# The first gate/up pair in seven products, and the last pair's forms beside the down units: a streaming encoder layer on one core

## The chip, the core and the metric

The kernel runs on one core of a Trainium2 chip. Its time is the device time of one execution in microseconds (us); of several runs the median is taken. A profile is one execution taken by the hardware profiler. The engines are TensorE (PE, with its weight loads as PEld), VectorE (DVE), ScalarE (ACT), GpSimd (POOL) and SyncE (SP), which here only issues DMAs. Every engine works through its own queue in order.

## The reference

One layer of an encoder trunk for 512 new prompt frames and 64 sample frames (576 columns in all), in fp32: a norm, an input projection, stick-breaking attention for eight heads beside a gated convolution, two output norms, an output projection with the residual, and then the part that the change touches:

```
h2 = rmsnorm(x, g_norm2)
x  = x + (silu(h2 @ w_gate) * (h2 @ w_up)) @ w_down      # D_MODEL 2048, D_FF 5632
```

The matrix products are held to fp32 accuracy. The kernel splits each operand into a high part (`float32r`) and a low part and takes three matmuls for each product of blocks: high x high, low x high, high x low.

## The kernel before

**Products.** Activations lie transposed: channels on the 128 partitions, the 576 frames in two halves of 288 (`HALVES`). A product of a weight block of 256 columns with all frames has two column tiles and two frame halves, and its rows come in pairs of tiles: a 2 x 2 by 2 x 2 block product. `run` computes it by seven products instead of eight (Winograd's form of Strassen's method). The products are numbered 1 to 7; products 1, 6, 5 and 3 accumulate in one bank (`psy`), 7 and 4 in another (`psw`), 2 in a third (`psx`). Between them ACT copies the bank (`kept`, line 428), so that a later addition can use the state at that point. One product over 2048 rows is 24 matmuls (8 row pairs x 3), so one unit is 168.

**Weights.** Raw columns come by DMA into two tiles of two halves each, `raw_a` and `raw_b` (`load_columns`, line 330), 1 MB a time. `weight_sums` (lines 347 to 353) forms the four sums of weight blocks on VectorE, and `prepare` splits one product's weights: a copy on ACT (line 231) and a subtraction on VectorE (line 232) into `whl`. It runs four products ahead.

**Frames.** The other operand of products 1, 2 and 3 are parts of the activations themselves (`h2a`, `b22s`); products 5 and 6 use the frame sums `t12`, products 7 and 4 the frame sums `t34`.

**Stages around the change.** `out_proj` runs twice: first over the convolution part, while the heads' attention runs between its steps, then over the attention part (799 to 901 us in the profile). In the second run each eviction multiplies by the row scale `Ra` and adds to the residual (lines 1005 and 1006), and `after_b2` makes the normed operand of the gate/up stage in high and low parts (lines 1248 and 1249) and sums squares (ACT line 1255, POOL line 1256). Then `wide` computes gate and up of the first column pair in eight products of 2 x 192 matmuls, with its own weight tiles, while `frame_sums` fills `t12` and `t34`. The row scale `R2` is formed in the middle of it (`row_scale2`). Then come 42 gate/up units (21 pairs) of seven products, then 37 down units. An activation `finish`es a gate or up quadrant: it is scaled by `R2`, the gate goes through Silu, and up is multiplied by gate.

**Forms.** The down units use seven products too, with the hidden activations as frames. So for each pair `put_forms` makes the seven frame forms (lines 1339, 231, 232) and stores each by DMA to `hid_dram` (line 1331, 288 KB), from SP, or from POOL for the last pair. `load_pair` brings a pair's forms back into one of seven slots (lines 1482 and 1490, 2 MB). The table `DOWN` says which row pairs a down unit covers: the first ones cover 3, 4, 5, 6 pairs, so a product of the first down unit is only 9 matmuls. The last pair's forms are first wanted by a unit near the end of the table.

**Order.** TensorE's order is written out by hand (`order`). Generators in a `Pipeline` advance at every step of three matmuls ("a tick"; `yield 9` waits nine). A planner sets the order on the other engines up to the last gate/up unit; from there on they follow the order of the text (`manual_schedule`).

Of the kernel before, what the change touches and what calls it, by code (L numbers as in the profile page):

```python
# [101 lines left out]
def tile_hybrid_stream_step(  # L102
# [47 lines left out]
    for w in (w_gate, w_up):  # L150
        for kk in range(2):
            specs.append((w[kk * 1024 : (kk + 1) * 1024, 0:256].rearrange("(k p) c -> p k c", p=P), 8, 256))
# [269 lines left out]
    def run(n, p_, early=False):  # L422
# [38 lines left out]
        elif p_ == 2:  # L461
            x = ps_z.tile([P, 512], F32, tag="z0", name="psx2")[:, :HALF]
            multiply(x, n, 2, True)
            add(0, 0, x, st["p1"])
# [531 lines left out]
    def out_proj(frame, R, after=None):  # L996
        for c in range(D // 256):
            whi, wlo = next_weight()
            load_x2()
            for j in range(2):  # L1000
                kt = 2 * c + j
                for a, b in HALVES:
                    ps = ps_pj.tile([P, HALF], F32, tag="pj", name="pjo")
                    product(ps, whi, wlo, slice(j * P, (j + 1) * P), frame, 8, a, b)
                    nc.vector.tensor_tensor(out=ps, in0=ps, in1=R[:, a:b], op=ALU.mult)
                    nc.vector.tensor_tensor(out=x2(kt)[:, a:b], in0=ps, in1=x2(kt)[:, a:b], op=ALU.add)
                if after:
                    after(kt)
# [225 lines left out]
    b12pool = tc.alloc_tile_pool(name="b12pool", bufs=1, reuse_waits="tile", side="left")  # L1234
    b12h = b12pool.tile([P, NP, HALF], F32R, name="b12h")
    b12l = b12pool.tile([P, NP, HALF], F32R, name="b12l")
    acc2 = [b12pool.tile([P, HALF], F32, name=f"acc2_{i}") for i in range(2)]

    def h2(kt, i):
        if i == 0:  # L1240
            return h2a[kt]
        return b22s[kt // 2] if kt % 2 else (b12h[:, kt // 2, :], b12l[:, kt // 2, :])

    def after_b2(kt):
        for i, (a, b) in enumerate(HALVES):
            hi, lo = h2(kt, i)
            src = x2(kt)[:, a:b]
            nc.scalar.activation(out=hi, in_=src, func=AF.Copy, scale=col("g2", kt))
            nc.vector.scalar_tensor_tensor(out=lo, in0=src, scalar=col("g2", kt), in1=hi.bitcast(F32),
                                           op0=ALU.mult, op1=ALU.subtract)  # L1250
# [6 lines left out]
        if kt % 4 == 3:  # L1257
            m = kt // 4
            for k in (4 * m, 4 * m + 2):
                nc.sync.dma_start(out=x2_dram[k : k + 2].rearrange("k p t -> p k t"), in_=x2t[k // 2])  # L1260

    out_proj(lambda k: mixa[k], Ra, after_b2)
    R2 = rpool.tile([P, T], F32, tag="R", name="R2", bufs=2)
    parts2 = []
    for i in range(2):
        sh, sl = parts("sq2")
        split(sh, sl, acc2[i])
        parts2.append((sh, sl))
# [13 lines left out]
    t34 = []  # L1282
# [5 lines left out]
    turn = [0]  # L1288

    def ps_tile(name):  # L1290
        turn[0] += 1
        if turn[0] % 2:
            return ps_pj.tile([P, HALF], F32, tag="pj", name=name)
        return ps_z.tile([P, 512], F32, tag=f"z{turn[0] // 2 % 3}", name=name)[:, :HALF]

    def frame_sums():

        for j in range(NP):
            ev, od = x2(2 * j), x2(2 * j + 1)
            ge, go = col("g2", 2 * j), col("g2", 2 * j + 1)  # L1300
            b11 = tmp.tile([P, HALF], F32, tag="ms", name="b11", bufs=1)
            b22 = tmp.tile([P, HALF], F32, tag="t", name="b22", bufs=1)
            nc.scalar.activation(out=b11, in_=ev[:, :HALF], func=AF.Copy, scale=ge)
            nc.scalar.activation(out=b22, in_=od[:, HALF:], func=AF.Copy, scale=go)
            ta = b12pool.tile([P, 2, HALF], F32, tag="ta", name="ta")
            tb = b12pool.tile([P, 2, HALF], F32, tag="tb", name="tb")
            t1, t2, t3, t4 = ta[:, 0], ta[:, 1], tb[:, 0], tb[:, 1]
            nc.vector.scalar_tensor_tensor(out=t1, in0=ev[:, HALF:], scalar=ge, in1=b11, op0=ALU.mult, op1=ALU.subtract)
            nc.gpsimd.tensor_tensor(out=t2, in0=b22, in1=t1, op=ALU.subtract)
            nc.vector.scalar_tensor_tensor(out=t3, in0=ev[:, HALF:], scalar=ge, in1=b22, op0=ALU.mult, op1=ALU.subtract)  # L1310
            nc.vector.scalar_tensor_tensor(out=t4, in0=od[:, :HALF], scalar=go, in1=t2, op0=ALU.mult, op1=ALU.subtract)
            two = t12[:, :, j] if j < NP - 1 else t12z
            split(two[:, :, 0, :], two[:, :, 1, :], ta)
            t34.append(ypool.tile([P, 2, 2, HALF], F32R, tag=f"y{j}", name=f"t34_{j}"))
            split(t34[j][:, :, 0, :], t34[j][:, :, 1, :], tb)
            yield 9

# [3 lines left out]
    spare = []  # L1321

    def put_form(fp, n, src):

        if fp == NFP - 1 and n > 3:
            t = spare.pop(0)()
        else:
            t = tmp.tile([P, 2, HALF], F32R, tag="hl", name="form")
# [28 lines left out]

    def finish(kind, fp, c, i, ps, part=None):
# [8 lines left out]
        else:  # L1367
            nc.vector.tensor_tensor(out=s, in0=ps, in1=part, op=ALU.add)  # L1368
            nc.vector.tensor_tensor(out=s, in0=s, in1=R2[:, a:b], op=ALU.mult)
        if kind == "gate":  # L1370
# [6 lines left out]
    def wide(kind, hold=None):  # L1377

        pss = {}
        for kk in range(2):  # L1380
            whi, wlo = next_weight()
            for i, j in ((1, 0), (1, 1), (0, 0), (0, 1)):
                if kk == 0:
                    pss[j, i] = ps_tile("pw")
                for k in range(8):
                    xh, xl = h2(8 * kk + k, i)
                    for n, (w_, x_) in enumerate(((whi, xh), (wlo, xh), (whi, xl))):
                        mm(pss[j, i], w_[:, k, j * P : (j + 1) * P], x_,  # L1388
                           start=(kk == 0 and k == 0 and n == 0), stop=(kk == 1 and k == 7 and n == 2))
                    pipe.tick()  # L1390
                if kk == 1:
                    finish(kind, 0, j, i, pss[j, i])
            if hold and kk == 0:
                hold()


    pipe.spawn(frame_sums(), 20)
    wanted += [(0, 0), (1, 0), (0, 1), (1, 1)] + [(n, c) for n in range(2, NGU) for c in range(2)]
    wanted += [(n, None) for n in range(NGU, NU)]
    wide("gate", row_scale2)  # L1400
    load_columns([("A", 0)])
    wide("up", lambda: load_columns([("A", 1)]))
    pipe.flush()
    b12pool.release()
# [3 lines left out]
    load_columns([("B", 0), ("B", 1)])  # L1408

# [191 lines left out]
```

## Time and profile before

| | |
|---|---|
| median of 3 runs | 2406.14 us (2406.02 to 2406.74) |
| profiled execution | 2408.49 us, span 2406.8 us |
| granted TensorE clock, mean | 0.994 |
| TensorE busy | 98% of the span, 17609 matmuls |
| VectorE, ScalarE, GpSimd busy | 81%, 51%, 12% |

A row of a group or of a timeline names line, engine, operation and tiles (written tile before the arrow, read tiles behind it) and the number of instructions. In a timeline the first number is the start and the second the time up to the end of the last instruction; matmuls follow each other more closely than they last, since they are pipelined. Square brackets give the idle time before and what ended it. In the table of stretches each engine has its busy time and number of instructions; the last columns are the granted clock, the DMA share and GB/s.

### The profile page before, as it was taken

The page shows a single profiled execution, that of the slowest core. Times are in us where ns is not written, and L with a number is a line of the kernel's source. Part 1 is how long each engine was busy: PE and PEld are TensorE (multiplying, and loading weights), DVE is VectorE, ACT ScalarE, POOL GpSimd, SP SyncE. Part 2 cuts the span into 40 slices and gives each one's busy share as a digit, 9 for nine tenths or more (in the row PEclk, how much of TensorE's full clock was granted, in tenths as well). Part 3 has the DMA queues.
Part 4 walks back from the last instruction along what each step waited for, and adds up shares of the span by engine and source line. Part 5 has one row for each costly group of instructions (what it writes and reads, how often), then busy time and mean ns, then how long its engine had stood idle before and what let it go on. Part 6 is the DMA issues. An engine that isn't in the chain of part 4 may idle for free.

```text
span 2406.8 us, 43812 instructions
## 1 busy us (share of the span) xinstructions
PE 2355.5 (98%) x17609; PEld 2339.5 (97%) x17609; DVE 1939.7 (81%) x2840; ACT 1235.0 (51%) x2207; POOL 298.9 (12%) x377
## 2 busy tenths in 40 slices
PE   8899999999999999999999999999999899999998
PEld 8899999998889999999999999999999899999998
DVE  7888898797677768888888888888888778887875
ACT  7456656455677545444444444444444444444454
POOL 0111121120233222000000000000000002431211
PEclk9999999999999999999999999999999999999999
DMA  7433342535632233535444444444444936885642
GB/s 253 140 113 108 108 140 86 161 99 184 224 107 89 100 127 118 155 112 158 150 128 145 146 143 132 144 150 141 129 152 141 339 112 205 221 226 195 205 128 79
DMA packets 474900, 360.60 MB, mean 150 GB/s; under 512 B 11278, under 2 KB 460680, under 8 KB 474696
## 3 DMA queue, kind: packets, MB, share of 16 engines
q1 hardware_dynamic: 469528, 351.02, 45.7%
q0 software_dynamic: 5168, 6.79, 1.6%
q8 instruction: 138, 2.26, 0.4%
q14 instruction: 66, 0.54, 0.1%
HBM read 281.39 MB, written 76.37 MB: 149 GB/s over the span
## 4 chain that ended last, share of the span: by engine, by line
PE 82%; DVE 6%; ACT 4%; issue 2%; POOL 2%; DMA 1%; SPq 0%; ACTq 0%; DVEq 0%; POOLq 0%
PE psy L405 43%; PE psw L405 21%; PE psx L405 10%; PE pjo L227 5%; DVE whl L232 1%; ACT whl L231 1%; PE pw L1388 1%; ACT ph L231 0%; PE psv L405 0%; PE pot L1511 0%; DVE c L866 0%; DVE raw_b L349 0%; POOL hbl L1117 0%; DMA raw_a<-in_w_down_dram 0%; DVE wlo L180 0%
## 5 line engine op out<-in xcount | busy, mean ns | idle before, releaser
L232 DVE TENSOR_TENSOR whl<-raw_a,whl 128x1024 fp32r<-128x1024 f32 (+4 forms) x376 | 426.4, 1135 | 69.4 <-ACT whl L231 67.8
L405 PE MATMUL psy<-t,whl 128*128 128x288 f32 x2916 | 438.4, 295 | 0.5 <-ACT part L428 0.5
L231 ACT CAST whl<-raw_a 128x1024 fp32r<-128x1024 f32 (+4 forms) x376 | 352.6, 938 | 137.9 <-PE psx L405 47.8
L405 PE MATMUL psy<-h_s,whl 128*128 128x288 f32 x2724 | 411.7, 295 | 6.8 <-ACT part L428 6.8
L405 PEld LDWEIGHTS psy<-t,whl 128*128 128x128 f32 x2916 | 403.7, 189 | 0.9 <-ACT part L428 0.7
L405 PEld LDWEIGHTS psy<-h_s,whl 128*128 128x128 f32 x2724 | 378.5, 189 | 7.3 <-ACT part L428 7.3
L405 PE MATMUL psw<-t,whl 128*128 128x288 f32 x2592 | 377.1, 295 | 0.0
L405 PEld LDWEIGHTS psw<-t,whl 128*128 128x128 f32 x2592 | 354.4, 189 | 0.2
L232 DVE TENSOR_TENSOR whl<-raw_b,whl 128x1024 fp32r<-128x1024 f32 (+5 forms) x230 | 248.7, 1081 | 86.4 <-ACT whl L231 85.1
L231 ACT CAST whl<-raw_b 128x1024 fp32r<-128x1024 f32 (+5 forms) x230 | 207.6, 904 | 206.9 <-PE psw L405 70.8
L428 ACT COPY part<-psy 128x288 f32<-128x288 f32 x303 | 121.2, 400 | 348.5 <-PE psy L405 346.4
L405 PE MATMUL psx<-h_s,whl 128*128 128x288 f32 x1122 | 165.1, 295 | 2.7 <-DVE gs L1368 2.7
L405 PEld LDWEIGHTS psx<-h_s,whl 128*128 128x128 f32 x1122 | 154.1, 188 | 2.9 <-issue 2.9
L231 ACT CAST whl<-s 128x1024 fp32r<-128x1024 f32 (+5 forms) x101 | 93.4, 924 | 119.9 <-PE psw L405 112.3
L405 PE MATMUL psy<-t12a,whl 128*128 128x288 f32 x1056 | 150.5, 295 | 3.1 <-ACT part L428 3.1
L405 PE MATMUL psw<-t34a,whl 128*128 128x288 f32 x1056 | 150.4, 295 | 2.1 <-DVE ghs L854 0.9
L405 PEld LDWEIGHTS psy<-t12a,whl 128*128 128x128 f32 x1056 | 143.5, 188 | 4.0 <-ACT part L428 4.0
L405 PEld LDWEIGHTS psw<-t34a,whl 128*128 128x128 f32 x1056 | 143.2, 188 | 2.7 <-DVE ghs L854 1.1
L227 PE MATMUL pjo<-mixc,whi 128*128 128x288 f32 x512 | 123.0, 307 | 1.2 <-ACT kcT L1063 1.2
L232 DVE TENSOR_TENSOR whl<-s,whl 128x1024 fp32r<-128x1024 f32 (+5 forms) x101 | 107.5, 1064 | 19.6 <-ACT whl L231 18.0
L1331 POOL DMA_DIRECT2D hid_dram<-form x3 | 2.4, 809 | 921.1 <-DVE form L232 921.1
L227 PE MATMUL pjo<-mixa,whi 128*128 128x288 f32 x512 | 102.1, 295 | 0.0
(599 smaller groups left out, 4146.8 us busy)
## 6 DMA issues: line engine op xcount, KB each, us to landing
hid_dram<-form SPq DMA_DIRECT2D x147, 288.0 KB, 2.3
raw_a<-in_w_gate_dram SPq DMA_DIRECT2D x23, 1024.0 KB, 6.2
raw_a<-in_w_up_dram SPq DMA_DIRECT2D x23, 1024.0 KB, 5.5
raw_a<-in_w_in_dram SPq DMA_DIRECT2D x22, 1024.0 KB, 5.5
raw_b<-in_w_in_dram SPq DMA_DIRECT2D x22, 1024.0 KB, 7.9
raw_b<-in_w_gate_dram SPq DMA_DIRECT2D x21, 1024.0 KB, 6.6
raw_b<-in_w_up_dram SPq DMA_DIRECT2D x21, 1024.0 KB, 7.7
h_s<-hid_dram SPq DMA_DIRECT2D x10, 2016.0 KB, 9.2
```

The lines of the kernel that those rows point to most:

```text
L227: mm(ps, w_[:, k, csl], x_[:, a:b], start=(k == 0 and n == 0), stop=(k == nk - 1 and n == 2))
L231: nc.scalar.copy(out=hi, in_=src)
L232: (lo_eng or nc.vector).tensor_tensor(out=lo, in0=src, in1=hi.bitcast(F32), op=ALU.subtract)
L405: mm(ps, whl[:, w_, j, :], x_, start=(start and j == 0 and q == 0), stop=(j == len(xs_) - 1 and q == 2), skip_group_check=True)
L428: nc.scalar.copy(out=t, in_=st["y"])
L1331: q.dma_start(out=hid_dram[fp][2 * n - 2 : 2 * n].rearrange("f p t -> p f t"), in_=t.bitcast(F32))
L1388: mm(pss[j, i], w_[:, k, j * P : (j + 1) * P], x_, start=(kk == 0 and k == 0 and n == 0), stop=(kk == 1 and k == 7 and n == 2))
```

## The change

The eight-product pair `wide`, its operand tiles and its weight loads go. All 22 pairs are units now, so there are 44 gate/up units. What they need at their start moves under the second `out_proj`:

- `frame_sums` is spawned for each pair of row tiles as soon as `out_proj` has finished it. `t34` goes where it went; `t12` cannot be written yet, as its memory still holds the attention operand, so each half goes to DRAM (`t12_dram`, 16 stores of 288 KB) and comes back in four loads when the projection has ended (`load_t12`).
- The columns of units 0 and 1 are loaded within the projection (`before_b2`), and the first two products of unit 0 are prepared there, with two of its weight sums.
- The start of `order` interleaves units 0 and 1, as the input projection's units do.
- `row_scale2` multiplies the sums of squares by ones in fp32 without splitting them, starts 19 ticks after the projection and takes the mean and the root in PSUM and on ACT. The first quadrant of unit 0 is finished six ticks late for it.
- For the last pair, `finish` leaves the quadrants that come last as they are, and `last_forms` does the rest: it starts 34 ticks later, beside the down units, and puts one form each ten ticks. The forms use the `hl` tiles instead of the down units' accumulators.

```diff
-    gu = [(kind, fp, 0, NP) for fp in range(1, NFP) for kind in ("gate", "up")]
+    gu = [(kind, fp, 0, NP) for fp in range(NFP) for kind in ("gate", "up")]
...
+    def frame_sums(j):
+        ev, od = x2(2 * j), x2(2 * j + 1)
...
+        nc.vector.scalar_tensor_tensor(out=t1, in0=ev[:, HALF:], scalar=ge, in1=b11, op0=ALU.mult, op1=ALU.subtract)
+        nc.gpsimd.tensor_tensor(out=t2, in0=b22, in1=t1, op=ALU.subtract)
+        nc.vector.scalar_tensor_tensor(out=t3, in0=ev[:, HALF:], scalar=ge, in1=b22, op0=ALU.mult, op1=ALU.subtract)
+        yield 4
+        nc.vector.scalar_tensor_tensor(out=t4, in0=od[:, :HALF], scalar=go, in1=t2, op0=ALU.mult, op1=ALU.subtract)
+        for q, t in enumerate((t1, t2)):
+            form = tmp.tile([P, 2, HALF], F32R, tag="hl", name="t12f")
+            split(form[:, 0], form[:, 1], t)
+            nc.sync.dma_start(out=t12_dram[q, j], in_=form.bitcast(F32))
+        yield 4
+        t34.append(ypool.tile([P, 2, 2, HALF], F32R, tag=f"y{j}", name=f"t34_{j}"))
+        for q, t in enumerate((t3, t4)):
+            split(t34[j][:, q, 0], t34[j][:, q, 1], t)
...
+        if kt % 2:
+            nc.sync.dma_start(out=x2_dram[kt - 1 : kt + 1].rearrange("k p t -> p k t"), in_=x2t[kt // 2])
+            pipe.spawn(frame_sums(kt // 2), 5)
+        if kt == KD - 2:
+            prepare(0, 1)
+            prepare(0, 2)
+            for _ in range(2):
+                one_sum(0)
+    def before_b2(c):
+        if c == 3:
+            load_columns([("B", 0), ("B", 1)])
+        elif c == D // 256 - 2:
+            load_columns([("A", 0)])
+        elif c == D // 256 - 1:
+            load_columns([("A", 1)])
...
     def row_scale2():
+        yield 19
         for i, (a, b) in enumerate(HALVES):
-            ss = channel_sums(*parts2[i], a, b, "ss2")
-            rsqrt_mean(R2[:, a:b], ss, D, HALF)
+            ss = misc("ss2")[:, :HALF]
+            mm(ss, oner.bitcast(F32), acc2[i], start=True, stop=True)
+            y, t = (tmp.tile([P, HALF], F32, tag=tag, name="y2") for tag in ("y", "r"))
+            nc.scalar.activation(out=ss, in_=ss, func=AF.Identity, scale=1.0 / D, bias=epsc)
+            nc.scalar.activation(out=y, in_=ss, func=AF.Ln)
+            nc.scalar.activation(out=y, in_=y, func=AF.Exp, scale=-0.5)
+            nc.scalar.activation(out=t, in_=y, func=AF.Square)
...
+    def load_t12():
+        yield 3
+        for q in (1, 0):
+            nc.sync.dma_start(out=t12[:, q].bitcast(F32), in_=t12_dram[q, : NP - 1].rearrange("j p f t -> p j f t"))
+            yield 6
+        for q in (1, 0):
+            nc.sync.dma_start(out=t12z[:, q].bitcast(F32), in_=t12_dram[q, NP - 1])
...
+    def last_forms(s10):
+        fp, h, tt = NFP - 1, hid.pop(NFP - 1), nc.vector.tensor_tensor
+        s00, s01, s11 = h[0, 0], h[0, 1], h[1, 1]
+        yield 34
+        tt(out=s01, in0=s01, in1=gates.pop((0, 1)), op=ALU.mult)
+        yield 5
+        tt(out=s10, in0=s10, in1=R2[:, :HALF], op=ALU.mult)
+        tt(out=s10, in0=s10, in1=gates.pop((1, 0)), op=ALU.mult)
+        for n, out, a, b in ((2, s10, None, None), (5, s00, s01, s00), (7, s01, s01, s11), (6, s11, s11, s00),
+                             (4, s10, s10, s11)):
+            yield 10
+            if a is not None:
+                tt(out=out, in0=a, in1=b, op=ALU.subtract)
+            put_form(fp, n, out)
...
-    wide("gate", row_scale2)
-    load_columns([("A", 0)])
-    wide("up", lambda: load_columns([("A", 1)]))
...
-    order = [(0, 1), (0, 2), (1, 1), (1, 2), (0, 6), (0, 7), (0, 5), (0, 3), (0, 4), (1, 6), (1, 7), (1, 5)]
-    for n in range(1, NU):
+    order = [(0, 1), (0, 2), (1, 1), (1, 2), (0, 3), (0, 6), (0, 5), (1, 3), (0, 7), (0, 4),
+             (1, 6), (1, 5), (1, 7), (2, 1), (1, 4), (2, 2), (2, 6), (2, 7), (2, 5)]
+    early = {0, 1}
+    for n in range(2, NU):
```

More of the change, by code (lines that the diff above doesn't have):

```diff
@@ L1442, in take_blocks @@
     def take_blocks(d):
+        if "z" not in down:
+            open_blocks()
         if d in (0, 3):
@@ L1534, in tile_hybrid_stream_step @@
     AHEAD = 4
-    for k_ in range(AHEAD):
+    for k_ in range(2, AHEAD):
         prepare(*order[k_])
```

140 lines of the change are left out of this document (48 added, 92 removed).

## The prediction, on record before the result was known

> **What bounds the kernel now.** I read the page first, then the busy time by stage, then the chain of waits, then the timelines of single engines where TensorE stands still.
>
> ```profile
> span 2406.8 us, 43812 instructions
> PE 2355.5 (98%) x17609; PEld 2339.5 (97%) x17609; DVE 1939.7 (81%) x2840; ACT 1235.0 (51%) x2207; POOL 298.9 (12%) x377
> PE 82%; DVE 6%; ACT 4%; issue 2%; POOL 2%; DMA 1%; SPq 0%; ACTq 0%; DVEq 0%; POOLq 0%
> ```
> TensorE is busy for 98% of the span and carries 82% of the chain. Work taken off VectorE, ScalarE or the DMA is worth only the TensorE time that waits for it, and a matmul taken away is worth its whole slot.
>
> ```profile
> 802.00:902.00 100.00, 100.00 (x756) 100.00 (x756) 71.95 (x138) 46.57 (x101) 24.43 (x30) 1.00 0.37 126
> 953.00:966.00 13.00, 10.31 (x78) 10.11 (x78) 12.97 (x16) 6.69 (x12) 5.09 (x4) 1.00 0.63 195
> 1060.00:1870.00 810.00, 810.00 (x6128) 810.00 (x6128) 679.51 (x928) 376.79 (x565) 0.00 (x0) 1.00 0.46 143
> 1870.00:1900.00 30.00, 23.69 (x174) 23.45 (x174) 20.53 (x37) 10.72 (x21) 5.34 (x7) 0.93 1.08 392
> ...
> 1898.00:1903.00 5.00, 4.62 (x20) 4.62 (x21) 3.91 (x8) 2.13 (x7) 0.73 (x1) 0.54 1.08 399
> ```
> The columns are stretch, length, then busy time of PE, weight load, DVE, ACT and POOL, granted clock, DMA share and GB/s. In the steady part of the gate/up units (1060 to 1870) TensorE never waits. It stands still at two places that the change touches: 2.69 us where the eight-product pair hands over to the units (953 to 966), and 6.31 us where the last gate/up unit hands over to the down units (1870 to 1900). After the second, its clock is 0.54 for five microseconds.
>
> ```profile
> 1080.49 9.52 PE psy L405 x72
> ...
> 1102.70 9.52 PE psy L405 x72
> ```
> These chain rows lie one unit of 168 matmuls apart: 22.21 / 168 = 0.1322 us for each 288-column matmul.
>
> **The change, part by part.**
>
> *Matmuls.* The first pair took 2 x 192 matmuls in eight products and takes 2 x 168 in seven. 48 x 0.1322 = 6.35 us less, all on the path.
>
> *Row scale.* Four fp32r matmuls against ones (0.53 us) become two fp32 ones, while the split of the sums goes.
>
> ```profile
> 780.69 0.38 PE L1141 MATMUL z<-pr,trir 128*128 128x128 f32 x2
> 780.91 0.39 PE L1142 MATMUL z<-pr,neg1r 128*128 128x128 f32 x2
> ```
> An fp32 matmul of 128 columns is two records and takes 0.22 us from start to start (780.69 to 780.91). At 288 columns it lies between two slots of 0.1322 (0.26) and the row scaled by columns (0.50), so two of them cost 0 to 0.46 more than now. I take 0.45, since the scaled row is the nearest of its kind. The square root chain on ACT and DVE starts 19 steps (7.5 us) after the projection and is first needed by an eviction three products later, so it is hidden; if it were late, the gate eviction in bank z0 and then TensorE would wait.
>
> *The start of the units.* Now:
>
> ```profile
> 952.83 2.94 PE L405 MATMUL psy<-h_s,whl 128*128 128x288 f32 x21
> ...
> 965.20 3.05 PE L405 MATMUL psx<-h_s,whl 128*128 128x288 f32 x21 [2.69 <-DVE gs L1368]
> ...
> 978.65 0.66 PE L405 MATMUL psy<-h_z,whl 128*128 128x288 f32 x3 [0.49 <-ACT part L428]
> ...
> 981.95 3.33 PE L405 MATMUL psw<-t,whl 128*128 128x288 f32 x24
> ```
> Eight products of 24 lie between 952.83 and 981.95: 29.12 us for 25.38, so 3.74 us are lost. Afterwards the order is the interleaved one that the input projection uses for its first two units, with the same banks:
>
> ```profile
> 98.51 3.34 PE L405 MATMUL psy<-t12a,whl 128*128 128x288 f32 x24
> 102.33 3.47 PE L405 MATMUL psy<-t12a,whl 128*128 128x288 f32 x24 [0.49 <-ACT part L428]
> ...
> 113.80 3.44 PE L405 MATMUL psw<-t34a,whl 128*128 128x288 f32 x24 [0.86 <-DVE ghs L854]
> ...
> 127.35 3.33 PE L405 MATMUL psy<-b,whl 128*128 128x288 f32 x24
> ```
> There eight products take 28.84 us for 25.38, so 3.46 us are lost: the third product into one bank waits for ACT's copy, the fourth product for an eviction. I take that: 0.28 us gained, with 0 to 7 us lost as the ends (nothing waits; or each of the two operands that VectorE finishes last is 1.5 us late on top).
>
> *Frame sums moved under the output projection.* Each of the eight column pairs of the projection's second half lasts 96 x 0.1322 = 12.7 us. VectorE's work in one pair, by these rows:
>
> ```profile
> L180 DVE TENSOR_TENSOR wlo<-raw_a,whi 128x512 fp32r<-128x512 f32 x30 | 24.2, 846 | 0.0
> L1005 DVE TENSOR_TENSOR pjo<-pjo,Ra 128x288 f32<-128x288 f32 x32 | 14.8, 461 | 12.6 <-PE pjo L227 12.5
> L1249 DVE SCALAR_TENSOR_TENSOR h_s<-x,vec,h_s 128x288 fp32r<-128x288 f32 x20 | 10.4, 518 | 7.5 <-ACT h_s L1248 7.5
> ...
> 838.83 1.28 DVE L180 TENSOR_TENSOR wlo<-raw_a,whi 128x512 fp32r<-128x512 f32 x2
> 840.09 0.52 DVE L1249 SCALAR_TENSOR_TENSOR h_s<-x,vec,h_s 128x288 fp32r<-128x288 f32 x1
> 840.52 1.90 DVE L180 TENSOR_TENSOR wlo<-raw_a,whi 128x512 fp32r<-128x512 f32 x2
> ...
> 840.46 0.81 POOL L1256 TENSOR_TENSOR acc<-acc,sq 128x288 f32<-128x288 f32 x1 [2.97 <-ACT sq L1255]
> ```
> Eight evictions at 0.46 (3.7), four weight pieces at 0.85 (3.4), three operand forms instead of four at 0.52 (1.6), and new: three sums at 0.52 (1.6) and four splits at about 0.46 (1.8). That is 12.1 us, and the order of the changed program puts two round trips to ACT of some 0.55 us behind a dependent pair. Independent instructions start closer than they last (840.09 to 840.52 is 0.43 for 0.52), about 1.5 us over 22 of them, so a pair takes near 11.7 of 12.7 us. TensorE has three banks; in that order the latest eviction is over about 3.4 us before its bank is needed. So I cost this at nothing; without that cover each microsecond beyond 12.7 costs one, seven times, less 3.4. ACT (46.6 of 100 us now) has room for six more short operations in each pair. POOL gets eight subtractions that it now runs later.
>
> Sixteen stores of 288 KB and two loads of 2 MB with two small ones are new on SP's queue:
>
> ```profile
> raw_a<-in_w_up_dram SPq DMA_DIRECT2D x23, 1024.0 KB, 5.5
> raw_b<-in_w_in_dram SPq DMA_DIRECT2D x22, 1024.0 KB, 7.9
> ...
> h_s<-hid_dram SPq DMA_DIRECT2D x10, 2016.0 KB, 9.2
> ```
> (last column: median us from issue to landing). The first 2 MB are asked for as the projection ends and needed five products (15.9 us) and the fp32 sums (1 us) later: 9.2 us fit. The other 2 MB and the two small loads stand on SP behind the store of the last form, which VectorE finishes about 8 us after the projection (some ten operations of 0.5 to 1.2 us stand before it); 8 + 9.2 and the small loads come to about 18, where the sixth product wants its last pair near 19.7. The weights of unit 2 queue behind them and are wanted later still. On POOL's queue the last pair's stores now wait for VectorE longer; behind them stand only additions of second visits, which start after eight units.
>
> *The hand-over to the down units.*
>
> ```profile
> 1889.52 0.96 PE L405 MATMUL psy<-h_s,whl 128*128 128x288 f32 x6
> ...
> 1891.51 0.56 PE L405 MATMUL psx<-t,whl 128*128 128x288 f32 x3
> 1898.38 1.81 PE L405 MATMUL psy<-h_s,whl 128*128 128x288 f32 x6 [6.31 <-ACT part L428]
> ...
> 1902.74 0.96 PE L405 MATMUL psy<-h_s,whl 128*128 128x288 f32 x6
> ...
> 1887.53 0.46 DVE L1339 TENSOR_TENSOR ut<-ux,ut 128x288 f32<-128x288 f32 x1
> ...
> 1891.53 0.55 DVE L349 TENSOR_TENSOR raw_a<-raw_a 128x384 f32<-128x384 f32 x1
> ```
> From 1889.52 to 1902.74 TensorE starts 36 matmuls: 13.22 us for 4.76, so 8.46 us are lost, 6.3 standing and 2.2 at the slow clock. The cause stands in VectorE's and ACT's queues: from 1887.53 three forms of the last pair, each a subtraction, an ACT copy and a split, before the weight sum at 1891.53, and two more behind it; ACT's copy of the first product's bank (L428) comes last of all. With the forms taken out, that sum starts at 1887.0 and the operand of the third product is split by 1889.3, before the product is due at 1891.9. The ACT copy is free at 1890.8, when its product ends. I leave 0.8 us for the rest: the forms come back ten steps (4 us) apart under the first down units, 12 VectorE operations of 0.46 and five waits of 0.5 for ACT, 8 us in 35; VectorE's idle share there is about a third. The ends are 0 and 4 us.
>
> The Trainium skill, page "TensorE: Matmul & The Clock Gate", section "What's actually happening", says that an idle window of about 3.4 us halves the array's clock until it has been busy as long. The trace agrees (clock 0.54 after 6.31 us); by it a gap cut to under 3.4 us also saves the slow stretch.
>
> *Sum.* -6.35 + 0.45 - 0.28 - 8.46 + 0.8 = -13.8 us. The profiled execution took 2408.49 us (span 2406.8 and 1.7 around it), 0.1% above the median of 2406.14; it becomes 2394.7, and the median 2392.3.
>
> **The rivals.**
>
> *VectorE sets the pace of the projection.* The pair at 840.52 shows it: 1.90 us for two weight pieces against 1.28, under a POOL addition of 0.81. Five POOL operations in each pair could slow the new splits as well. If three of them do by 0.6 us each, a pair takes 13.5 us; 7 x 0.8 - 3.4 = 2.2, and with one round trip more near 4: 2396. Against it: the evictions, which read PSUM, keep 461 ns in the mean of all 32, so only part of the queue is open to it.
>
> The Trainium skill, page "SBUF — State Buffer", speaks against the change here: VectorE operations with two SBUF inputs and POOL operations lock one port pair and block each other for a whole instruction. Applied to every such operation it is this rival, and by it 2396.
>
> *The gap stays, for another reason.* DMA is full (1.08) from 1870 to 1903 with the slots of the down units. If the next slot and not the forms ends the wait, only 1 of 8.46 us goes: 2406.14 - 6.2 = 2400. Against it: TensorE had read three slots by 1891.5 without waiting.
>
> *The other side.* In the changed order the weight sum of unit 0 stands in VectorE's queue ahead of the row scale Ra and of the projection's first evictions, and it waits for a 1 MB load.
>
> ```profile
> 799.07 0.29 PE L227 MATMUL pjo<-mixa,whi 128*128 128x288 f32 x1
> ...
> 804.42 0.46 DVE L281 SCALAR_TENSOR_TENSOR Ra<-t,y 128x288 f32<-128x288 f32 x1
> ...
> 805.65 0.46 DVE L1006 TENSOR_TENSOR x<-pjo,x 128x288 f32<-128x288 f32 x1
> ...
> 1874.63 1.22 DVE L353 TENSOR_TENSOR raw_a<-raw_a 128x1024 f32<-128x1024 f32 x1
> ```
> The second half starts at 799.07; its first bank is free at 806.1 and wanted at 809.1 (three products and 0.5 for the sums). The weight sum, 1.22 us by its like, would run at 804.4 and leaves 1.8 us of this. If the load lands after 806.2, TensorE waits one for one: the gain of 13.8 is gone at 820, and the kernel is slower by 0.2% at 825. The load can start at 799; loads of this size take 5.5 to 7.9 us here, so this needs one held back in the queue.
>
> **How the numbers follow.** Forecast 0.58 (2392), VectorE at its limit 0.17 (2396), gap stays 0.11 (2400), the late load or a like wait 0.14, half of it within 0.2% and half beyond. 0.2% (4.8 us) is about what a measurement tells from no change. The forecast's own range is 2389.5 (fp32 sums free, no remainder at the hand-over, half of the 3.46 us at the start) to 2396; the whole range reaches to 2400. Faster 0.86, same 0.07, slower 0.07.
>
> **What would show it.** Right: no eight-product group, 7392 gate/up matmuls, no TensorE idle above 1 us near 1890, clock 1.00 there, no TensorE wait in the projection. Wrong: waits for a bank or a weight piece in the projection, for t12 in the sixth product, or for VectorE among the first five down units.

## The result and the profile after

The changed kernel takes 2400.37 us in the median of 11 runs (2398.56 to 2402.97), the kernel before 2406.7 us in 11 runs beside them: ratio 0.9975, 95% interval 0.9966 to 0.9984. Run once more with the later experiments it came to 0.9966 (0.9954 to 0.9979). So it is faster by 0.25 to 0.34%, 6 to 8 us, where 13.8 us were forecast; 2400.37 us lies outside the forecast's own range (2389.5 to 2396) and just beyond the end of the whole one (2400). The profiled execution took 2402.2 us, 6.3 less than that of before.

The page of the changed kernel, and its busy time by stage (stretch, length, busy time of PE, weight load, DVE, ACT and POOL, granted clock, DMA share, GB/s):

```profile
span 2400.5 us, 43832 instructions
PE 2351.3 (98%) x17561; PEld 2334.0 (97%) x17561; DVE 1952.9 (81%) x2856; ACT 1238.8 (52%) x2221; POOL 299.8 (12%) x377
```

```profile
802.00:902.00 100.00, 100.00 (x757) 100.00 (x757) 90.50 (x174) 56.82 (x127) 32.08 (x35) 1.00 0.53 178
902.00:953.00 51.00, 45.60 (x323) 44.22 (x322) 40.24 (x55) 25.56 (x43) 3.75 (x4) 0.97 0.62 203
...
938.00:941.00 3.00, 2.85 (x12) 2.85 (x13) 2.73 (x4) 0.44 (x1) 0.00 (x0) 0.50 0.04 13
1900.00:1905.00 5.00, 5.00 (x40) 5.00 (x39) 4.34 (x8) 2.27 (x5) 0.00 (x0) 1.00 1.08 389
```

There are 48 matmuls fewer. In the output projection TensorE never waits although VectorE is now busy for 90.5 of 100 us. At 1900, where the clock was 0.54, it is 1.00. But from 902 to 953, the first products of the units, TensorE stands for 5.4 us, and runs for another three at half its clock. TensorE's timeline shows where (start, time up to the end of the last matmul; in brackets the idle time before and what ended it):

```profile
902.66 2.96 PE L401 MATMUL psy<-h_s,whl 128*128 128x288 f32 x21
...
910.62 1.13 PE L1312 MATMUL ss<-acc,oner 128*128 128x288 f32 x4
...
912.77 0.56 PE L401 MATMUL psy<-h_z,whl 128*128 128x288 f32 x3
...
923.21 0.67 PE L401 MATMUL psy<-t12z,whl 128*128 128x288 f32 x3 [0.76 <-DMA t12z<-t_dram]
924.66 3.08 PE L401 MATMUL psy<-t,whl 128*128 128x288 f32 x21 [0.78 <-ACT part L424]
928.86 0.67 PE L401 MATMUL psv<-h_z,whl 128*128 128x288 f32 x3 [0.72 <-ACT part L424]
938.15 4.82 PE L401 MATMUL psw<-t,whl 128*128 128x288 f32 x24 [2.65 <-DVE gs L1405]
...
953.09 2.94 PE L401 MATMUL psy<-h_s,whl 128*128 128x288 f32 x21
...
1889.22 0.95 PE L401 MATMUL psy<-h_s,whl 128*128 128x288 f32 x6
1917.42 1.09 PE L401 MATMUL psy<-h_s,whl 128*128 128x288 f32 x6 [0.67 <-ACT part L424]
...
2274.65 0.92 PE L401 MATMUL psx<-t,whl 128*128 128x288 f32 x5 [0.24 <-DVE whl L228]
```

Four of these rows are marks that every kernel with the new start has: the first gate/up matmul (902.66), the first product of unit 2 (953.09, thirteen products later), the first down matmul (1889.22), and a late wait for a weight piece (2274.65), which before stands at 2281.75. The first gate/up matmul of before:

```profile
901.35 0.29 PE L1388 MATMUL pw<-b12h,whi 128*128 128x288 f32 x1
...
2281.75 0.92 PE L405 MATMUL psx<-t,whl 128*128 128x288 f32 x5 [0.25 <-DVE whl L232]
```

From the first gate/up to the first down matmul the kernel before takes 1889.52 - 901.35 = 988.17 us, the changed one 986.56: only 1.61 us less, where 6.18 were forecast. From there to the late mark it is 392.23 against 385.43 us: 6.80 less, where 7.66 were forecast. The remaining +2.1 us of this pair of executions lie outside both stretches: 1.3 ahead of the first gate/up matmul, which came between 897.8 and 902.7 us in the executions of this study, and 0.8 behind the late mark. So the stretches tell more than the spans. All runs by them, each from one profiled execution (ratio: median to before, beside runs of before on the same chip):

| kernel | ratio, interval | first gate/up to unit 2 | first gate/up to first down | first down to late mark |
|---|---|---|---|---|
| before | 1 | | 988.17 | 392.23 |
| changed | 0.9975 (0.9966 to 0.9984) | 50.43 | 986.56 | 385.43 |
| after_again | 0.9966 (0.9954 to 0.9979) | 51.00 | 987.14 | 385.17 |
| front_only | 0.9999 (0.9990 to 1.0008) | 53.68 | 989.81 | 392.06 |
| forms_only | 0.9968 (0.9956 to 0.9979) | | 988.12 | 384.96 |
| manual | 0.9994 (0.9986 to 1.0003) | 47.39 | 991.49 | 384.87 |
| reorder | 0.9951 (0.9939 to 0.9964) | 48.15 | 984.28 | 384.98 |
| direct | 0.9961 (0.9947 to 0.9974) | 49.79 | 985.93 | 384.88 |
| store_first | 0.9964 (0.9951 to 0.9976) | 48.48 | 984.61 | 385.40 |
| all3 | 0.9945 (0.9933 to 0.9958) | 45.28 | 981.41 | 384.01 |
| front_fixed | 0.9971 (0.9959 to 0.9983) | 45.48 | 981.61 | 391.39 |
| all4 | 0.9929 (0.9917 to 0.9942) | 43.04 | 979.17 | 385.53 |
| apart | 0.9925 (0.9911 to 0.9939) | 42.99 | 979.12 | 382.95 |

Thirteen products without a wait would take 13 x 24 x 0.1322 = 41.2 us. From unit 2 on, every kernel with the new start except manual takes the same 936.1 us to the first down matmul (986.56 - 50.43, and so on). What differs between them differs in the first thirteen products. A row of the table is one execution, and the ratio rests on all of them: the profiled executions of all3, store_first and after_again were 3.4, 2.3 and 1.9 us faster than the medians of these runs. So the stretches tell where the time of an execution went, and the ratios what an edit is worth.

### The profile page after: what moved, and what is told of

Its sections match the earlier page's. It is cut to its first block, busy times and chain, and to the rows that moved or that the text cites. A ratio compares the mean times of both kernels' runs of the same rounds, so it can differ in the third digit from the quotient of the medians.

```text
span 2400.5 us, 43832 instructions
## 1 busy us (share of the span) xinstructions
PE 2351.3 (98%) x17561; PEld 2334.0 (97%) x17561; DVE 1952.9 (81%) x2856; ACT 1238.8 (52%) x2221; POOL 299.8 (12%) x377
## 4 chain that ended last, share of the span: by engine, by line
PE 79%; DVE 8%; ACT 4%; issue 2%; DMA 2%; POOL 1%; SPq 0%; DVEq 0%; ACTq 0%; POOLq 0%
PE psy L401 44%; PE psw L401 22%; PE psx L401 10%; DVE whl L228 1%; DVE wlo L176 1%; PE pjo L223 1%; DVE pjo L1010 1%; DVE x L1011 0%; DMA raw_b<-in_w_gate_dram 0%; ACT whl L227 0%; ACT ph L227 0%; PE psv L401 0%; PE pot L1514 0%; DVE c L869 0%; DVE h_s L1280 0%
## 5 line engine op out<-in xcount | busy, mean ns | idle before, releaser
L228 DVE TENSOR_TENSOR whl<-raw_a,whl 128x1024 fp32r<-128x1024 f32 (+4 forms) x384 | 436.0, 1136 | 67.8 <-ACT whl L227 66.0
L401 PE MATMUL psy<-t,whl 128*128 128x288 f32 x3000 | 449.7, 295 | 1.8 <-ACT part L424 1.8
L227 ACT CAST whl<-raw_a 128x1024 fp32r<-128x1024 f32 (+4 forms) x384 | 360.2, 940 | 144.5 <-PE psx L401 46.8
L401 PE MATMUL psy<-h_s,whl 128*128 128x288 f32 x2766 | 417.7, 295 | 1.6 <-ACT part L424 1.6
L401 PEld LDWEIGHTS psy<-t,whl 128*128 128x128 f32 x3000 | 413.9, 188 | 2.6 <-ACT part L424 2.5
L401 PE MATMUL psw<-t,whl 128*128 128x288 f32 x2688 | 391.7, 295 | 2.6 <-DVE gs L1405 2.6
L401 PEld LDWEIGHTS psw<-t,whl 128*128 128x128 f32 x2688 | 368.3, 189 | 3.0 <-DVE gs L1405 2.9
L228 DVE TENSOR_TENSOR whl<-raw_b,whl 128x1024 fp32r<-128x1024 f32 (+5 forms) x234 | 254.3, 1087 | 88.3 <-ACT whl L227 87.2
L401 PE MATMUL psx<-h_s,whl 128*128 128x288 f32 x1164 | 170.7, 294 | 0.0
L401 PEld LDWEIGHTS psx<-h_s,whl 128*128 128x128 f32 x1164 | 159.5, 188 | 0.0
```

Of the source, the lines that this page charges most:

```text
L227: nc.scalar.copy(out=hi, in_=src)
L228: (lo_eng or nc.vector).tensor_tensor(out=lo, in0=src, in1=hi.bitcast(F32), op=ALU.subtract)
L401: mm(ps, whl[:, w_, j, :], x_, start=(start and j == 0 and q == 0), stop=(j == len(xs_) - 1 and q == 2), skip_group_check=True)
```

## The experiments

**One part alone.** `front_only` takes the second part of the change away:

```diff
-            if kind == "up" and fp == NFP - 1 and (c, i) == (1, 0):
-                pipe.spawn(last_forms(s))
-                return
...
+        if fp == NFP - 1 and n > 3:
+            t = spare.pop(0)()
```

> The change without its second part: all pairs by seven products and the fp32 row scale, the last pair's forms as before. Theory (the start of the units took back most of what the 48 matmuls gave: from the first to the last gate/up matmul the changed kernel is only 1.6 us shorter): 1.6 us faster than before, ratio 0.9993, inside what a measurement tells from nothing, the 6.3 us of standing TensorE at the hand-over there again, and the same waits of 0.8, 0.8, 0.7 and 2.7 us at 923 to 938. Rival (the start is as short as predicted and the second part is worth nothing on its own): 6.2 us faster, ratio 0.9974.

Ratio 0.9999: 48 matmuls fewer gave nothing. TensorE's timeline of it has longer waits than the changed kernel, and the idle of 6.30 us near 1890:

```profile
922.11 0.67 PE L401 MATMUL psy<-t12z,whl 128*128 128x288 f32 x3 [2.85 <-DMA t12z<-t_dram]
923.26 4.58 PE L401 MATMUL psy<-t,whl 128*128 128x288 f32 x21 [0.49 <-ACT part L424]
...
938.25 4.76 PE L401 MATMUL psw<-t,whl 128*128 128x288 f32 x24 [2.90 <-DVE gs L1395]
...
1898.13 1.81 PE L401 MATMUL psy<-h_s,whl 128*128 128x288 f32 x6 [6.30 <-ACT part L424]
```

The theory stands and the rival falls; that even the 1.6 us were gone was expected by neither (the wait for `t12z` is 2.1 us longer here, and half clock follows twice).

`forms_only` is the kernel before with `last_forms` and the `hl` tiles for the last forms, and nothing else:

> The kernel before with the second part of the change alone: the last column pair's forms ten steps apart beside the down units, pair 0 still by eight products. Theory (the hand-over is worth 6.8 us, whatever the start does): ratio 0.9972, no idle of 6.3 us near 1890, clock 1.00 there, two waits of about half a microsecond for ACT's copies in the 30 us that follow. Rival (the gap closes only because the units start otherwise): ratio 0.9990 or nearer 1.

Ratio 0.9968; from the first down matmul to the late mark 7.27 us less than before, and up to there as long as before (988.12). One of the two waits came (0.42 us at 1920.64), and one of 0.77 at 2047.85. Around the hand-over TensorE stands for these 0.42 us only, at full clock:

```profile
1860.00:1930.00 70.00, 69.58 (x524) 69.12 (x523) 52.99 (x87) 32.63 (x61) 5.33 (x7) 1.00 0.92 319
```

So the second part is worth 7 us by itself (8.4 in the medians), which is all or nearly all that the changed kernel gains.

**The queue of VectorE.** In the changed kernel's VectorE and SyncE timelines around the longest wait:

```profile
936.50 1.23 DVE L343 TENSOR_TENSOR s<-raw_b 128x1024 f32<-128x1024 f32 x1 [1.77 <-DMA raw_b<-in_w_gate_dram]
937.64 0.45 DVE L1405 TENSOR_TENSOR gs<-psw,part 128x288 f32<-128x288 f32 x1
```

```profile
929.99 0.37 SPq L326 DMA_DIRECT2D raw_b<-in_w_gate_dram  x1
```

Product (0,7) has filled its bank by 935.5, and the eviction that empties it for (0,4) could run. Ahead of it in VectorE's queue stands the first weight sum of unit 2, which waits until 936.5 for columns that could only be asked for at 929.99, when the last split from their half of `raw_b` was done. `manual` writes VectorE's order out for ten products, so that the sum stands later:

```diff
+        if k_ == 6:
+            start.enter_context(tc.manual_schedule(engines={mybir.EngineType.DVE}))
+        if k_ == 16:
+            start.close()
```

> The changed kernel with VectorE's order written out from the seventh to the sixteenth product, so that the weight sum of unit 2, which waits for a load, no longer stands ahead of the gate eviction that frees the bank for product (0,4). Theory (that one place costs 2.8 us of standing and 1.5 us at half clock): the wait at 938 shrinks from 2.65 to about 0.7 us, the clock stays at 1.00, and the kernel is 3.6 us faster than the changed one: ratio to before 0.9960. Rival (VectorE is full in these 20 us, and another eviction or weight piece is late instead): no more than 1 us, ratio 0.9971 to 0.9977, with a new wait for VectorE of 2 us or more between 930 and 960.

TensorE's timeline of manual, then VectorE's:

```profile
934.08 3.47 PE L401 MATMUL psw<-t,whl 128*128 128x288 f32 x24 [0.55 <-DVE gs L1405]
...
960.90 0.61 PE L401 MATMUL psy<-t,whl 128*128 128x288 f32 x1 [3.54 <-ACT whl L227]
```

```profile
933.56 0.46 DVE L1405 TENSOR_TENSOR gs<-psw,part 128x288 f32<-128x288 f32 x1 [0.81 <-PE psw L401]
...
955.02 0.46 DVE L228 TENSOR_TENSOR form<-ut,form 128x288 fp32r<-128x288 f32 x1 [1.49 <-ACT form L227]
955.40 1.22 DVE L343 TENSOR_TENSOR s<-raw_b 128x1024 f32<-128x1024 f32 x1
```

At the place in question the theory holds: the eviction runs when its bank is full, the wait is 0.55 us and no half clock follows (3.47 us for 24 matmuls, 4.82 in the changed kernel); the first thirteen products take 3.0 us less. (How much of the 3.0 is due to the order is open: in the changed kernel run again, below, the same wait is 0.91 us without any edit.) The total does not: 0.9994 in place of 0.9960. In the written order the sums of unit 2 came only at 955.40, behind forms that wait for ScalarE, and (2,6) waited 3.54 us for its weights, with half clock behind it; from unit 2 to the first down matmul this kernel takes 8 us more than the others. A wait as long as the rival named came, but VectorE was not full: it stood for 1.5 us ahead of the sums.

`reorder` leaves the queues to the planner and changes which product follows which:

```diff
-    ... (0, 3), (0, 6), (0, 5), (1, 3), (0, 7), (0, 4), (1, 6), (1, 5), (1, 7), (2, 1), ...
+    ... (0, 3), (0, 7), (0, 6), (0, 5), (1, 3), (0, 4), (1, 6), (1, 7), (1, 5), (2, 1), ...
```

> The changed kernel with the first products in another order: (0,7) ahead of (0,6), (1,3) between (0,5) and (0,4), (1,7) ahead of (1,5). No product now follows another in bank z1, and the operand of the sixth frame sum is wanted 3.2 us later. Theory: the waits for the last frame pair (0.76), for the eviction (2.65, with the 1.5 us of slow clock) and for ACT's third copy (0.49) go, the copies between (0,6), (0,5) and (1,3) stay: 5.4 us faster than the changed kernel, ratio to before 0.9952. Rival (VectorE is full): the same work is late at other products, ratio 0.9965 to 0.9975.

Ratio 0.9951, as the theory has it: the waits for the eviction and for `t12z` are gone. That the number fits so well is in part luck: up to the first down matmul this execution is only 2.3 us ahead of the changed kernel's, where 5.4 were expected. Two copies on ScalarE were later than expected (1.68 and 2.05 us, the second with half clock behind it). TensorE's timeline, then ScalarE's:

```profile
930.88 0.67 PE L401 MATMUL psv<-h_z,whl 128*128 128x288 f32 x3 [2.05 <-ACT part L424]
```

```profile
915.11 0.77 ACT L227 CAST t<-tb 128x288 fp32r<-128x288 f32 x2 [3.32 <-DMA x_dram<-x]
...
923.63 0.43 ACT L227 CAST form<-ut 128x288 fp32r<-128x288 f32 x1 [2.50 <-DVE ut L1416]
...
928.54 1.99 ACT L227 CAST whl<-raw_a 128x1024 fp32r<-128x1024 f32 x2 [3.23 <-DVE raw_a L349]
```

Right ahead of the two copies stand a form's split and two weight pieces that wait for VectorE. Ten microseconds earlier ScalarE waits to write the last frame sums until the store of `x` from the same memory has landed. The changed kernel has this wait too, shorter (1.26 us). That it made VectorE late is argued here, not shown.

**Three waits one by one.** The changed kernel again, beside the next three:

> The changed kernel once more, beside the three that follow. Both theories: ratio to before 0.9975 as before. What it is for: how far the start differs from one profiled execution to the next. If the wait for the last frame pair's operand is set by when its load lands (theory), it is long (2 to 3 us) where the output projection ends early and short where it ends late; if it is set by VectorE (rival), it is 0.8 us again.

The first gate/up matmul came at 897.79, early, and the wait for the operand's load was 2.30 us, against 0.76 where it came at 902.66 (and 2.85 in front_only at 899.47). So what differs from one execution to the next is the load's landing, not VectorE, which finished the operand's last part 10.6 us (after_again) and 10.7 us (changed kernel) after the first gate/up matmul:

```profile
907.91 0.44 DVE L228 TENSOR_TENSOR t12f<-ta,t12f 128x288 fp32r<-128x288 f32 x1
```

```profile
912.94 0.44 DVE L228 TENSOR_TENSOR t12f<-ta,t12f 128x288 fp32r<-128x288 f32 x1
```

The wait for the eviction differs as much: 2.65 us in the changed kernel, 0.91 us here, where the columns of unit 2 had landed before their sum was due.

`direct` splits the last pair's frame sums straight into `t12z`, which is free by then:

```diff
+            if j == NP - 1:
+                split(t12z[:, q, 0], t12z[:, q, 1], t)
+                continue
...
-        for q in (1, 0):
-            nc.sync.dma_start(out=t12z[:, q].bitcast(F32), in_=t12_dram[q, NP - 1])
```

> The changed kernel with the last frame pair's two operands split straight into their place in SBUF, without the store to DRAM and the load back. Theory (the round trip costs product (0,6) 0.8 to 2.9 us): that wait goes; the gate eviction's wait at 938 stays, and takes part of it: 1.0 to 2.0 us faster than the changed kernel, ratio 0.9967 to 0.9971. Rival (VectorE is full until 931 and the weight load of unit 2 after it, so that an earlier sixth product only waits longer later): ratio 0.9975.

Ratio 0.9961, beyond the theory's range on the fast side: 1.7 us less than after_again in the medians (the two intervals overlap), 0.6 and 1.2 us less than the two executions of the changed kernel up to the first down matmul. The wait for the load is gone, that for the eviction stays:

```profile
934.81 4.96 PE L401 MATMUL psw<-t,whl 128*128 128x288 f32 x24 [2.58 <-DVE gs L1406]
```

`store_first` holds SyncE to the order of the text for two products, which puts the last store of `x` ahead of the 2 MB load:

```diff
+        if kt == KD - 1:
+            stores.enter_context(tc.manual_schedule(engines={mybir.EngineType.SP}))
...
+        if k_ == 2:
+            stores.close()
```

> The changed kernel with the last store of x put ahead of the first 2 MB load of the frame sums in SyncE's queue. Theory (that store lands only behind the load, 8 to 10 us after it is asked for; ScalarE's split of the last frame sums waits for its buffer, and with it the square root chain and VectorE, which is full afterwards): ScalarE's idle of 1.3 us and more ahead of that split goes, VectorE's work is earlier by it, the weight load of unit 2 too, and the wait at 938 is shorter by as much; the first load lands 2 us later, which the sixth product may feel by up to 1 us. 1.0 to 2.5 us faster than the changed kernel, ratio 0.9965 to 0.9971. Rival (the later load costs the sixth product what ScalarE gains): ratio 0.9973 to 0.9980.

ScalarE's timeline, first of the changed kernel run again, then of store_first, and TensorE's of store_first:

```profile
911.54 0.77 ACT L227 CAST t<-tb 128x288 fp32r<-128x288 f32 x2 [2.48 <-DMA x_dram<-x]
```

```profile
908.53 0.77 ACT L227 CAST t<-tb 128x288 fp32r<-128x288 f32 x2 [0.36 <-DVE tb L1264]
```

```profile
933.88 3.44 PE L401 MATMUL psw<-t,whl 128*128 128x288 f32 x24 [0.91 <-DVE gs L1409]
```

ScalarE's wait is gone, and up to the first down matmul this execution is 2.0 and 2.5 us shorter than the two of the changed kernel. But TensorE's waits are those of after_again: 2.42 us for `t12z` and 0.91 for the eviction, against 2.30 and 0.91. What differs from after_again is the clock, which stayed at 1.00 (last section). In the medians the difference is 0.6 us, which these runs cannot tell from nothing, and 0.9964 lies just outside the theory's range. So that the store costs TensorE time is not shown by this run.

**Together.** `all3` is reorder, direct and store_first in one.

> The order of products of the run reorder, the straight split of the last pair and the store of x ahead of the loads, together. Theory (the start loses its time to these three waits and to the slow clock behind them, and to nothing else above the copies): two or three waits of 0.5 to 0.9 us for ScalarE's copies are left, the clock stays at 1.00, the first thirteen products lose 2.5 us in place of 6.9 in reorder: ratio to before 0.9933. Rival (VectorE is full, so that the products wait for weight pieces or evictions instead): ratio 0.9948 to 0.9955, with waits for VectorE of 1 us and more.

Ratio 0.9945. The clock stays at 1.00 and the thirteen products take 45.28 us, the time that the forecast's terms make (41.2 + 1.0 for the fp32 sums + 3.46 = 45.7). But the ratio lies on the rival's side, and one wait is longer than the theory had it: 1.99 us for ScalarE's copy between (0,6) and (0,5). TensorE's timeline, then ScalarE's:

```profile
924.48 3.05 PE L401 MATMUL psy<-t,whl 128*128 128x288 f32 x21 [1.99 <-ACT part L424]
```

```profile
923.09 1.04 ACT L227 CAST whl<-raw_a 128x1024 fp32r<-128x1024 f32 x1 [2.52 <-DVE raw_a L349]
```

No product waits for VectorE itself, but the copy stands behind a weight piece that does, so VectorE's part in it is not excluded. Nor does that wait alone explain the ratio: the profiled execution, which has it, took 2391.47 us, 0.9933 of the median of before.

`front_fixed` is front_only with the same three edits, so without the later forms:

> The run front_only (pair 0 by seven products, the last pair's forms as before) with the three edits of all3. Theory (the 48 matmuls are worth what was forecast, 6.2 us, once the waits of the start are gone; all3 went from the first to the last gate/up matmul in 981.4 us against 988.2 before): first gate/up to first down matmul 981.4 us, the idle of 6.3 us near 1890 there again, 6.8 us faster than before, ratio 0.9972. Rival (all3 owes its gain to the room that the later forms leave, or to something else after the start): 985 us or more between these two matmuls, ratio 0.9985 or nearer 1.

Ratio 0.9971, 981.61 us between the two matmuls and 6.31 us of idle near 1890:

```profile
1891.84 1.81 PE L401 MATMUL psy<-h_s,whl 128*128 128x288 f32 x6 [6.31 <-ACT part L424]
```

The first part of the change is worth 6.9 us in the medians (2407.86 to 2400.95) when its start is in order, and nothing that could be measured as it was built. The rival falls.

`all4` puts (0,7) between (0,6) and (0,5), which share a bank:

```diff
-             ... (0, 3), (0, 7), (0, 6), (0, 5), ...
+             ... (0, 3), (0, 6), (0, 7), (0, 5), ...
```

> all3 with (0,6) ahead of (0,7), so that (0,7) stands between the two products that use one bank one after the other. Theory (the 2.0 us that product (0,5) waits for ScalarE's copy in all3 are the copy behind a weight piece that waits for VectorE; one product in between covers them): no wait above 0.6 us in the start, 1.5 to 2 us faster than all3, ratio to before 0.9937. Rival (the weight piece and the sums are late whatever stands between, and the wait moves to product (1,3) or (0,4)): ratio 0.9945.

2391.99 us, ratio 0.9929. One wait is left in the first thirteen products, and they take 43.04 us, 2.2 less than in all3; VectorE is busy for 46.73 of 51 us and holds no product up:

```profile
900.49 2.97 PE L401 MATMUL psy<-h_s,whl 128*128 128x288 f32 x21
927.57 0.66 PE L401 MATMUL psv<-h_z,whl 128*128 128x288 f32 x3 [0.49 <-ACT part L424]
943.53 2.94 PE L401 MATMUL psy<-h_s,whl 128*128 128x288 f32 x21
```

```profile
902.00:953.00 51.00, 50.51 (x379) 50.06 (x378) 46.73 (x65) 30.49 (x51) 7.28 (x6) 1.00 0.58 193
```

**The rest of the hand-over.** In the changed kernel ScalarE's timeline ahead of the wait at 1917.42:

```profile
1916.63 0.43 ACT L227 CAST form<-ut 128x288 fp32r<-128x288 f32 x1 [2.26 <-DVE ut L1392]
1916.97 0.39 ACT L424 COPY part<-psy 128x288 f32<-128x288 f32 x1
```

A form's split stands ahead of the bank copy, and waits for a subtraction that VectorE does behind a weight sum. `apart` is all4 with the subtraction seven steps ahead of the split:

```diff
-            yield 10
+            yield 3
             if a is not None:
                 tt(out=out, in0=a, in1=b, op=ALU.subtract)
+            yield 7
             put_form(fp, n, out)
```

> all4 with each subtraction of the last forms seven steps (2.8 us) ahead of the form's split and store instead of in the same step; ScalarE's order is as in all4. Theory (the 1.3 us that the down units still wait for ScalarE near 1908 and 1913 come from a form's split that stands in ScalarE's queue ahead of the bank copy and waits for the subtraction, which VectorE does late): both waits shrink below 0.3 us together, first down matmul to the matmul that waits for a weight piece 0.25 us near 2264 is 384.2 us against 385.5 in all4, ratio to before 0.9924. Rival (the copy is late because of the weight pieces ahead of it, which wait for their loads): both waits stay, 385.5 us, ratio 0.9929.

Both waits are gone. The first down matmul and the late mark:

```profile
1879.29 0.96 PE L401 MATMUL psy<-h_s,whl 128*128 128x288 f32 x6
...
2262.24 0.92 PE L401 MATMUL psx<-t,whl 128*128 128x288 f32 x5 [0.24 <-DVE whl L228]
```

The stretch is 382.95 us, 2.6 less than in all4, twice what was expected. A third wait of all4, 0.41 us at 2039.99, has gone as well; 0.9 us of the difference is not accounted for. This is the fastest version: 2389.2 us (2388.47 to 2391.03), ratio 0.9925 (0.9911 to 0.9939). Against all4 alone the medians differ by 2.8 us, but were not taken side by side.

## Why the prediction was half right

**Matmuls (-6.35) and row scale (+0.45): right.** From unit 2 on, every kernel with the new start except manual takes the same 936.1 us for 295 products of 24, which is 0.1322 us for each matmul. The two fp32 sums and the rest of the product around them take 912.77 - 910.62 = 2.15 us for 9 x 0.1322 = 1.19: 0.96 us, 0.43 more than the 0.53 of before.

**The start of the units (-0.28): the step that failed.** It was taken by analogy with the first units of the input projection. Up to the first down matmul the changed kernel gains 1.61 and 1.03 us in its two executions; less the two terms above, the start cost 4.3 and 4.9 us more than the old one (7.5 in front_only). In the prediction's own count, the time lost over the slots, it took 3.46 us, with 0 to 7 as the ends, against 3.74 before; 8.0 and 8.6 us were lost (11.3 in front_only), more than the worse end. What the analogy left out:

- VectorE's weight sum of unit 2, which waits for a load ahead of the gate eviction: 2.65 us of standing and 4.66 - 3.17 = 1.5 us of half clock in the changed kernel (0.91 us of standing in after_again, 2.90 in front_only). The prediction saw this kind of wait and placed it a hundred microseconds earlier, at the row scale Ra, where it did not come. The same load was dismissed in a clause ("wanted later still").
- The last frame pair's round trip through DRAM. It was to be back 18 us after the projection and wanted at 19.7. It came 20.6 us after it (923.21 - 902.66), and 22.1 and 22.6 us in after_again and front_only. In the changed kernel about the whole excess over 18 arose before the trip: the last form, put at some 8 us behind the projection, was finished by VectorE at 10.7.
- The last store of `x`. It was in no term of the sum: it lands behind the first 2 MB load, 8.02 us after it is asked for, and ScalarE waits for its memory. The chain of waits that ends in the 2.65 us of the changed kernel has it, but what it cost TensorE is not shown, since with that store moved TensorE's waits were as in after_again:

```profile
907.25 8.02 DMA x_dram<-x
```

With all three mended (all3, front_fixed) the stretch takes 981.4 and 981.6 us, where the prediction's terms give 982.0. The match is close in part by chance: all3 loses its 3 us at other places than the input projection, and all4 goes down to 979.17. Which share each of the three had is not separated. But the arithmetic of TensorE was sound, and what failed was the cover: each of the three is a piece of work that stands behind something late in a queue.

**The projection (0): right.** Nothing waits there at 90.5% of VectorE. So the rival in which VectorE sets its pace falls, and with it, for these instructions, the result of 2396 that the Trainium skill's page "SBUF — State Buffer" (section "SBUF: two separate sides") was drawn on for: POOL is busy for 32 of these 100 us, and TensorE does not wait. Whether VectorE and POOL blocked each other below that limit, this does not tell.

**The hand-over (-8.46 + 0.8): right in kind.** 6.8 and 7.1 us in the changed kernel, so the rest is 1.4 to 1.7 us in place of 0.8. The prediction's reason for a rest, waits of VectorE for ScalarE, was turned round: it was ScalarE that waited for VectorE, with a bank copy behind it, and `apart` removes it. The rival that the gap stays for another reason falls: DMA is as full as before (1.08 at 1900), and TensorE runs. That the result came out at 2400 us, the time of this rival, is chance: the gap closed, and the start lost what it gave. (The rival's 2400 also leaves out the 1 us that it says would go.)

**The clock.** By the Trainium skill, page "TensorE: Matmul & The Clock Gate", section "What's actually happening", an idle window of about 3.4 us puts the clock down, and the prediction took from it that a shorter gap would save the slow stretch. The trace does not agree: 2.65 us of idle at 938 were followed by three microseconds at 0.50.

## What to carry to other kernels

When a stage's start is moved, an analogy with another stage gives the matmuls and the bank conflicts, but not the queues: list for each in-order engine what it will wait for in the new order, and ask what stands behind that. Short products in the same bank one after the other, a small store issued behind a large load, and a prefetch's first use put ahead of an eviction each made an engine stand for one to three microseconds here, and order alone took each of these waits away (though manual shows that a new order can bring a longer one). Two parts that a change brings together should be timed apart: here one was worth 7 us and the other nothing until its start was mended, and the sum alone could have been read as half of each.

## What the runs showed of the hardware

The clock does not follow the length of an idle alone. TensorE dropped to 0.50 after 2.65 us of idle (changed kernel, at 938), after 2.30 (after_again, where the clock was down before the 0.49 that followed), and about a microsecond after an idle of 2.05 (reorder, with 1.68 one product earlier); it stayed at 1.00 after 2.69 us in the kernel before (965.20) and after 2.42 and 0.49 in store_first. The stretches of after_again and then of store_first, where the idles are nearly alike:

```profile
920.00:923.00 3.00, 2.51 (x9) 2.16 (x10) 3.00 (x5) 1.14 (x3) 0.00 (x0) 0.50 0.62 199
```

```profile
921.00:924.00 3.00, 2.29 (x15) 2.05 (x16) 2.95 (x3) 2.07 (x3) 0.00 (x0) 1.00 1.14 353
```

The same page of the Trainium skill, same section, says that activity is judged over a window that runs freely. That would let the same idle fall either way; no run here tells where such a window begins, so the cause stays open. For a sum on this kernel it means that an idle of 2 to 3 us is to be priced with and without some 1.5 to 2 us of slow clock behind it.

The store of `x` landed 3.3 us after its issue in store_first, and 8.02 us in the changed kernel, where a 2 MB load had been issued on the same queue just before it.
